# A decoder trunk on one core: the two compressions of a sparse attention done as one, and new constants in the clock that orders TensorE's work

## The chip, the cores and the metric

The kernel runs on 1 core of one Trainium2 chip. The metric is the device time in microseconds, lower is better. Three runs of the kernel before took 1984.06 to 1987.67 us, with a median of 1984.88 us.

## The reference

Four decoder layers over 256 positions of width 1024, float32. Each layer is a half-step SwiGLU FFN (width 2816), a token mixer, and a second FFN, each between RMS norms with a residual. Layers 0 and 3 have windowed attention, layer 2 a block attention, and layer 1 the sparse attention that the change touches. Its compressed branch makes one key and one value out of every 32 positions (stride 16, 15 blocks, 4 groups of heads):

```python
def compress_kv(kv, pos, w1, w2):
    B, S, G, dh = kv.shape                       # 1, 256, 4, 64
    n_cmp = (S - CMP_LEN) // CMP_STRIDE + 1      # 15
    idx = jnp.arange(n_cmp)[:, None] * CMP_STRIDE + jnp.arange(CMP_LEN)[None, :]
    blocks = kv[:, idx] + pos[:, None, :]
    flat = blocks.transpose(0, 1, 3, 2, 4).reshape(B, n_cmp, G, CMP_LEN * dh)
    return jax.nn.gelu(flat @ w1) @ w2           # w1: 2048 x 256, w2: 256 x 64

kc_b = compress_kv(kc, cmp_pos[0], cmp_w1[0], cmp_w2[0])
vc_b = compress_kv(vc, cmp_pos[1], cmp_w1[1], cmp_w2[1])
# p_cmp = masked_softmax(q . kc_b);  o_cmp = p_cmp @ vc_b
# o = g0 * o_cmp + g1 * o_selected + g2 * o_window
```

## The kernel before, in words

**Two chains.** The 256 positions are two tiles of 128 rows, and each has a chain of steps (class `Chain`, t = 0 and 1) through all four layers. A step is a Python generator's stretch between two `yield`s, and the steps of the two chains are laid one behind the other on TensorE. Both chains use the same weights: a slab (1 MB, two halves of 128x1024 floats) serves chain 0 and then chain 1.

**Weights.** Every half is loaded by SyncE into one of four `raw` buffers, and split: ScalarE writes `hi` (rounded to fp32r), VectorE writes `lo` = raw - hi. A product with a slab half is then x_hi*hi, x_hi*lo and x_lo*hi; 12 products of 512 columns are one visit of a chain to a slab. `hi` and `lo` go into a pool of 28 slots (`SLOTS`, `k4`), which the attention's tiles share. `plan.held` counts the slots that four users hold (chain 0, chain 1, the keys and values, and the compression, which is number 3), `plan.want` what is reserved for them, and `room()` what is left; `feed()` splits the next half only where two slots are left and 1.2 us (`PACE`) have passed on the rough clock.

**The rough clock.** TensorE's order is the order in which the program emits its instructions (`manual_schedule`), and `choose()` decides it: among the steps of the two chains and of the helpers that are running, the one whose inputs are ready first, ties going to the lower rank (the compression has rank -1, chain 0 rank 0, chain 1 rank 1, the compressed core rank 1.5). What is ready when comes from class `Clock`: every emitted instruction moves it on by a fixed duration that stands in `TimedProducts.matmul` (L226) and `Engines` (L252 to L257). The orders on ScalarE, VectorE and SyncE come from the compiler's own scheduler, which takes the emitted order as priority. An instruction of TensorE that is placed too early waits on the chip, and all behind it waits too.

**The sparse layer** (`attn_b`, L888). Each chain projects queries, gates and six kinds of keys and values (ten visits and a product of 48 columns), then runs `core`: eight jobs of four heads, in each the scores (`acc<-k,k`), a maximum on VectorE, exp on ScalarE, transposes (`trp`), and the product with the values (`pv`). When chain 1 has the first half of its keys, `compress()` (L946) is started beside the cores. It takes the keys (s = 0), and then the values (s = 1): four adds on VectorE lay out the blocks in `xf` (`k<-k,post`), 16 products of 256 columns with w1 come in four steps of four (`hid`; the weights `k<-w` come in quarters, each into a slot), then a GELU of seven instructions on 64 partitions, two transposes (`hidT`), and the small second product (`kcb`, `vcb`). When both are there, `cmp_core` (L849) of both chains may go on (`scc`, `trc`, `pvc`).

A float32 product is two records on TensorE, one fp32r product or one transpose is one. A hidden product has 64 output rows: it uses half of the array's columns (the form `128*64`).

Of the kernel before, what the change touches and what calls it, by code (L numbers as in the profile page):

```python
# [214 lines left out]
class TimedProducts:  # L215
# [7 lines left out]
    def matmul(self, out, lhs, rhs, share=1.0, **kw):  # L223
        c, n = self.clock, free_size(rhs)
        self.begin(out, lhs, rhs)
        c.now += share * (max(0.107, n / 2372) if rhs.dtype == F32R else max(0.213, n / 600))  # L226
        c.passed(c.now, [out], [lhs, rhs])
        self.engine.matmul(out, lhs, rhs, **kw)  # L228

# [21 lines left out]
class Engines:  # L251
    def __init__(self, nc, clock):  # L252
        self.tensor = TimedProducts(nc.tensor, clock)
        self.scalar = Timed(nc.scalar, "act", clock, 0.06, 0.00083)
        self.vector = Timed(nc.vector, "dve", clock, 0.065, 0.00105)
        self.gpsimd = Timed(nc.gpsimd, "pool", clock, 0.45, 0.001)
        self.sync = TimedLoads(nc.sync, clock)  # L257
# [3 lines left out]
def trunk(ctx: ExitStack, tc: tile.TileContext, x, rel, gains, pre, sinks, pos, w1, w2, wts, hot,  # L261
# [43 lines left out]
    def drop(who, n=1):  # L305
        plan.held[who] -= n

    def k2(shape, dtype=F32):
        return p2.tile(shape, dtype, tag="k2", name="k2")
# [103 lines left out]
    class Chain:  # L413
# [474 lines left out]
        def attn_b(self, i):  # L888
            t = self.t
            r, r8 = self.r_and_r8()  # L890
            if t == 0:
                shared["cmp"] = False
                shared["cT"] = [k4(2, [P, 4, SEQ]) for _ in range(2)]
                shared["kT"] = k4(2, [P, 2, 2, SEQ])
                shared["v"] = k4(2, [P, 2, 2, 256])
            kT, vs = shared["kT"], shared["v"]
            yield from self.queries(r8)
            p = yield from self.project(48)
            gate = self.small("gate", 48)
            rh = self.small("rh")  # L900
            nc.vector.tensor_scalar_mul(rh, r, 0.5)
            nc.scalar.activation(gate, p[:, :48], AF.Tanh, scale=rh)
            nc.vector.tensor_scalar(gate, gate, 1.0, 0.5, op0=ALU.add, op1=ALU.mult)
            gate = gate.rearrange("p (h b) -> p b h", b=3)
            yield free_bank(), True
            p = yield from self.project(512)
            for s in range(2):
                self.keys_dup(p[:, s * 256:(s + 1) * 256], r, shared["cT"][s])
            yield from self.turns()
            plan.want[t] = 3 + 2 * t  # L910
            for s in range(2):
                p = yield from self.project(512)
                self.keys(p[:, :256], r, kT[:, s, :, t * P:(t + 1) * P])
                nc.scalar.activation(vs[:, t, s, :], p[:, 256:], AF.Copy, scale=r)
                if t == 0 and s == 0:
                    plan.want[3] = 3
                yield from self.turns(s == 1)
                if t and s == 0:
                    start(compress(), FIRST)
            o = k4(t, [P, D])  # L920
            branches = [(lambda h, s=s: kT[:, s, h // 8, :],
                         lambda h, kb, s=s: vs[:, kb, s, (2 * (h // 8) + h % 2) * DH:
                                               (2 * (h // 8) + h % 2 + 1) * DH],
                         gate[:, s + 1, :]) for s in range(2)]
            self.oc = k4(t, [P, D])
            self.cmp = False
            start(self.cmp_core(gate[:, 0, :]), CMP_CORE)
            yield from self.core(o, branches, 0)
            while not self.cmp:
                yield clock.now + 0.5, False  # L930
            for q in range(2):
                c = slice(q * 512, (q + 1) * 512)
                nc.vector.tensor_add(o[:, c], o[:, c], self.oc[:, c])
            drop(t)
            self.leave(3)
            yield from self.out_proj(o, i)
# [8 lines left out]

    def compress():  # L946

        vbd = k4(2, [P, 2, 8, DH])
        nc.vector.memset(kcb, 0.0)
        hv = k2([P, 2, 2, 4, 32])  # L950
        for s in range(2):
            src = shared["cT"][s]
            xf = k4(3, [P, 16, 4, 16])
            nc.vector.memset(xf[:, :, :, NCMP:], 0.0)
            view = src.rearrange("p g (n j b) -> p j g n b", j=8, b=2)
            for e in range(2):
                rows = slice(DH * e, DH * e + DH)
                for m in range(2):
                    nc.vector.tensor_tensor(
                        xf[rows, 8 * m:8 * m + 8, :, :NCMP], view[rows, :, :, m:m + NCMP, e],  # L960
                        post[rows, s, 8 * m:8 * m + 8].unsqueeze(2).unsqueeze(3)
                        .broadcast_to([DH, 8, 4, NCMP]), op=ALU.add)
            drop(2)
            plan.want[2] -= 1
            ws = []
            for q in range(2):
                w = k4(3, [P, HALF])
                nc.sync.dma_start(w, w1[2 * s, :, q * HALF:(q + 1) * HALF])
                ws.append(w)
            p = bank([64, 2, P], "hid")  # L970
            for q in range(4):
                w = ws[q]
                yield when(w, xf), False
                for j in range(4 * q, 4 * q + 4):
                    at = (j % 4) * CMP_HIDDEN
                    nc.tensor.matmul(p.rearrange("p c n -> p (c n)"),
                                     xf[:, j].rearrange("p g n -> p (g n)"),
                                     w[:, at:at + CMP_HIDDEN], start=j == 0, stop=j == 15)
                drop(3)
                if q < 2:  # L980
                    w = k4(3, [P, HALF])
                    nc.sync.dma_start(w, w1[2 * s + 1, :, q * HALF:(q + 1) * HALF])
                    ws.append(w)
            drop(3)
            hid = k2([64, 2, P])
            q = k2([64, 2, P])
            nc.scalar.activation(q, p, AF.Square)
            nc.vector.tensor_scalar(q, q, 0.044715, 1.0, op0=ALU.mult, op1=ALU.add)
            nc.vector.tensor_tensor(q, q, p, op=ALU.mult)
            nc.scalar.activation(q, q, AF.Tanh, scale=GELU_C)  # L990
            nc.vector.tensor_scalar(q, q, 1.0, 0.5, op0=ALU.add, op1=ALU.mult)
            nc.vector.tensor_tensor(hid, q, p, op=ALU.mult)
            yield max(when(hid), free_bank()), False
            p = bank([P, 2, 64], "hidT")
            for c in range(2):
                nc.tensor.transpose(p[:, c, :], hid[:, c, :], ident[:64, :64])
            hid = k2([P, 2, 64])
            nc.vector.tensor_copy(hid, p)
            if s == 0:
                yield max(when(hid), free_bank()), False  # L1000
                p = bank([P, 64], "kcb")
                for c in range(2):
                    nc.tensor.matmul(p, w2s[:, 0, c].rearrange("p a d -> p (a d)"), hid[:, c, :],
                                     start=c == 0, stop=c == 1)
                for e in range(2):
                    rows = slice(DH * e, DH * e + DH)
                    nc.vector.tensor_copy(
                        kcb[rows, :, e, :],
                        p[rows, :].rearrange("p (g e n) -> p g e n", e=2, n=16)[:, :, e, :])
            else:  # L1010
                for c in range(2):
                    nc.vector.tensor_copy(
                        hv[:, c], hid[:, c, :].rearrange("p (g n) -> p g n", n=32).unsqueeze(2)
                        .broadcast_to([P, 2, 4, 32]))
                for G in range(2):
                    yield max(when(hv), free_bank()), False
                    p = bank([P, DH], "vcb")
                    for c in range(2):
                        nc.tensor.matmul(p, hv[:, c, G].rearrange("p a n -> p (a n)"),
                                         w2s[:, 1, c, 0, :], start=c == 0, stop=c == 1)  # L1020
                    nc.vector.tensor_tensor(vbd[:, G], p.unsqueeze(1).broadcast_to([P, 8, DH]),
                                            bm.unsqueeze(2).broadcast_to([P, 8, DH]), op=ALU.mult)
        shared["vbd"] = vbd
        plan.want[3] = 0
        shared["cmp"] = True
# [84 lines left out]
```

## Time and profile before

| what | value |
|---|---|
| median of three runs | 1984.88 us (1984.06 to 1987.67) |
| profiled execution | 1989.9 us |
| its span, first to last instruction | 1988.1 us |
| TensorE busy, share of the span | 1947.6 us, 98% |
| VectorE busy, share | 1236.2 us, 62% |
| ScalarE busy, share | 1040.7 us, 52% |
| GpSimd busy, share | 37.1 us, 2% |
| mean granted TensorE clock | 0.996 |

Products overlap in the records (one of 512 columns is shown with 389 ns, and the next starts 227 ns after it), so TensorE's busy share says where it waited long, and not how close to its peak it is. What a product costs is read from the start of one to the start of the next.

### The profile page before, as it was taken

To read this page: it belongs to the slowest core of one execution; us is meant where nothing else is said; L and a number is where in the kernel's file an instruction comes from. 1 tells how busy PE (TensorE), PEld (TensorE's weight loads), DVE (VectorE), ACT (ScalarE), POOL (GpSimd) and SP (SyncE) were. 2 spreads that over 40 slices of the span, in tenths; PEclk is the share of its full clock that TensorE was granted. 3 is DMA by queue.
4 is the path that set the end of the run, shared out by engine and by line. 5 is a ranking of instruction groups with operands and counts; after the bars stand their busy time and mean duration, and the time that the engine had idled before them with its cause. 6 is when DMAs were issued, how large, how long until landed. Compare 5 with 4: busy or idle time off the path is not lost. (4 is left out here: it accounts for less than half of the span.)

```text
span 1988.1 us, 27346 instructions
## 1 busy us (share of the span) xinstructions
PE 1947.6 (98%) x9948; PEld 1589.5 (80%) x9948; DVE 1236.2 (62%) x2271; ACT 1040.7 (52%) x1886; POOL 37.1 (2%) x62
## 2 busy tenths in 40 slices
PE   7999999999999999999999999999999999999998
PEld 6778878888888886788888887778888888878886
DVE  6556676556655648765566556466556655667553
ACT  6445665445544555554455446565445544665442
POOL 0000000000000000000000000000000000000000
PEclk9999999999999999999999999999999999999999
DMA  8578556555555454365555555556555555536551
GB/s 265 172 230 238 173 143 199 190 188 184 191 190 191 141 180 109 119 199 191 185 183 193 188 184 179 178 147 201 184 186 186 195 185 185 177 106 207 188 184 57
DMA packets 114099, 356.42 MB, mean 179 GB/s; under 512 B 12811, under 2 KB 30475, under 8 KB 113964
## 3 DMA queue, kind: packets, MB, share of 16 engines
q1 hardware_dynamic: 113964, 354.68, 55.3%
q8 instruction: 78, 1.28, 0.2%
q14 instruction: 57, 0.47, 0.1%
HBM read 352.01 MB, written 2.62 MB: 178 GB/s over the span
## 5 line engine op out<-in xcount | busy, mean ns | idle before, releaser
L210 DVE TENSOR_TENSOR lo<-raw,hi 128x1024 fp32r<-128x1024 f32 x625 | 761.0, 1223 | 378.0 <-ACT hi L210 346.9
L210 ACT ACTIVATE hi<-raw 128x1024 fp32r<-128x1024 f32 x625 | 660.6, 1064 | 383.4 <-PE acc L228 202.1
L228 PE MATMUL proj<-hi,xh 128*128 128x512 f32 (+1 forms) x1696 | 675.7, 400 | 2.6 <-DVE xl L210 1.9
L228 PE MATMUL proj<-lo,xh 128*128 128x512 f32 (+1 forms) x1696 | 658.7, 389 | 0.8 <-DVE lo L210 0.8
L228 PE MATMUL proj<-hi,xl 128*128 128x512 f32 (+1 forms) x1696 | 449.2, 387 | 0.0
L228 PEld LDWEIGHTS proj<-hi,xh 128*128 128x128 f32 x1696 | 320.6, 189 | 64.4 <-ACT xh L210 3.0
L228 PEld LDWEIGHTS proj<-lo,xh 128*128 128x128 f32 x1696 | 321.2, 189 | 61.5 <-DVE lo L210 1.1
L228 PEld LDWEIGHTS proj<-hi,xl 128*128 128x128 f32 x1696 | 316.2, 188 | 67.7
L228 PE MATMUL acc<-hi,hh 128*128 128x512 f32 x704 | 219.5, 393 | 3.0 <-ACT hh L210 3.0
L228 PE MATMUL acc<-lo,hh 128*128 128x512 f32 x704 | 217.7, 390 | 0.0
L228 PE MATMUL acc<-hi,hl 128*128 128x512 f32 x704 | 188.8, 390 | 0.0
L210 ACT ACTIVATE h<-proj,rh 128x256 f32<-128x256 f32 x176 | 82.0, 466 | 189.7 <-PE proj L228 189.6
L210 ACT ACTIVATE hh<-trh 128x256 fp32r<-128x256 f32 x176 | 66.9, 380 | 177.7 <-PE trh L235 177.6
L228 PEld LDWEIGHTS acc<-hi,hh 128*128 128x128 f32 x704 | 131.3, 189 | 30.1 <-ACT hh L210 3.7
L228 PEld LDWEIGHTS acc<-lo,hh 128*128 128x128 f32 x704 | 132.7, 189 | 27.9
L228 PEld LDWEIGHTS acc<-hi,hl 128*128 128x128 f32 x704 | 132.2, 188 | 27.7
L210 DVE SCALAR_TENSOR_TENSOR h<-h,proj 128x256 f32<-128x256 f32 x176 | 73.6, 418 | 120.0 <-ACT h L210 119.9
L210 DVE TENSOR_TENSOR hl<-trh,hh 128x256 fp32r<-128x256 f32 x176 | 73.9, 420 | 112.2 <-ACT hh L210 112.2
L210 ACT ACTIVATE k<-k,nm 128x128 f32<-128x128 f32 (+1 forms) x160 | 70.7, 446 | 35.8 <-DVE nm L210 35.7
L210 DVE SCALAR_TENSOR_TENSOR h<-proj,c,h 128x256 f32<-128x256 f32 x176 | 85.0, 483 | 5.2
L235 PE MATMUL trh<-ident,h 128*128 128x128 f32 x352 | 67.0, 272 | 0.0
L235 PEld LDWEIGHTS trh<-ident,h 128*128 128x128 f32 x352 | 48.7, 139 | 22.4 <-PE tab L228 0.6
(100 smaller groups left out, 1116.3 us busy)
## 6 DMA issues: line engine op xcount, KB each, us to landing
raw<-wts SPq DMA_DIRECT2D x624, 512.0 KB, 4.5
bias<-scratch SPq DMA_DIRECT2D x96, 128.0 KB, 5.0
g<-gains SPq DMA_DIRECT2D x12, 512.0 KB, 4.9
k<-w SPq DMA_DIRECT2D x8, 512.0 KB, 6.0
scratch<-k SPq DMA_DIRECT2D x4, 384.0 KB
out<-x SPq DMA_DIRECT2D x4, 256.0 KB, 2.1
x<-x SPq DMA_DIRECT2D x2, 256.0 KB
x<-x SPq DMA_DIRECT2D x1, 512.0 KB
```

The costliest lines, as they stand in the source:

```text
L210: return call(out, *args, **kw)
L228: self.engine.matmul(out, lhs, rhs, **kw)
L235: self.engine.transpose(out, src, ident)
```

## The change

The two compressions are done together, and the first product in two parts. Both layouts `xf` are made first (eight adds), and each part takes half of w1's rows for keys and values: 16 products, one for the keys and one for the values in turn, into the two halves of a bank's partitions. The rough clock counts each with half of its duration (`share=0.5`). The first part's sums are copied out by ScalarE, the second's added to them by VectorE; then one GELU runs on 128 partitions, with two transposes of 128x128, and the second products as before. The compression may now hold 6 slots (two `xf` and four quarters) in place of 3. The waits for the inputs come once for each part, with all four quarters.

In the rough clock an fp32r product of 512 columns goes from 0.2158 to 0.2268 us, a float32 one of 256 columns from 0.4267 to 0.4324 us, and an instruction of ScalarE on 1024 columns from 0.910 to 0.964 us. VectorE's, GpSimd's and the loads' constants stay.

```diff
@@ class TimedProducts
-        c.now += share * (max(0.107, n / 2372) if rhs.dtype == F32R else max(0.213, n / 600))
+        c.now += share * (max(0.112, 0.0135 + n / 2400) if rhs.dtype == F32R else max(0.22, n / 592))
@@ class Engines
-        self.scalar = Timed(nc.scalar, "act", clock, 0.06, 0.00083)
+        self.scalar = Timed(nc.scalar, "act", clock, 0.07, 0.000873)
@@ attn_b
                 if t == 0 and s == 0:
-                    plan.want[3] = 3
+                    plan.want[3] = 6
@@ compress
         hv = k2([P, 2, 2, 4, 32])
+        xfs = []
         for s in range(2):
             src = shared["cT"][s]
             xf = k4(3, [P, 16, 4, 16])
...
+            xfs.append(xf)
             drop(2)
             plan.want[2] -= 1
-            ws = []
-            for q in range(2):
+        ws = []
+
+        def quarter(q):
+            for s in range(2):
                 w = k4(3, [P, HALF])
-                nc.sync.dma_start(w, w1[2 * s, :, q * HALF:(q + 1) * HALF])
+                nc.sync.dma_start(w, w1[2 * s + q // 2, :, q % 2 * HALF:(q % 2 + 1) * HALF])
                 ws.append(w)
-            p = bank([64, 2, P], "hid")
-            for q in range(4):
-                w = ws[q]
-                yield when(w, xf), False
-                for j in range(4 * q, 4 * q + 4):
-                    at = (j % 4) * CMP_HIDDEN
-                    nc.tensor.matmul(p.rearrange("p c n -> p (c n)"),
-                                     xf[:, j].rearrange("p g n -> p (g n)"),
-                                     w[:, at:at + CMP_HIDDEN], start=j == 0, stop=j == 15)
-                drop(3)
-                if q < 2:
-                    w = k4(3, [P, HALF])
-                    nc.sync.dma_start(w, w1[2 * s + 1, :, q * HALF:(q + 1) * HALF])
-                    ws.append(w)
-            drop(3)
-            hid = k2([64, 2, P])
...
+        sums = []
+        for m in range(2):
+            quarter(2 * m)
+            quarter(2 * m + 1)
+            yield max(when(*ws[4 * m:], *xfs), free_bank()), False
+            p = bank([P, 2, P], "hid")
+            for j in range(8):
+                at = (j % 4) * CMP_HIDDEN
+                for s in range(2):
+                    nc.tensor.matmul(p[HALVES[s]].rearrange("p c n -> p (c n)"),
+                                     xfs[s][:, 8 * m + j].rearrange("p g n -> p (g n)"),
+                                     ws[4 * m + j // 4 * 2 + s][:, at:at + CMP_HIDDEN], share=0.5,
+                                     start=j == 0, stop=j == 7)
+            drop(3, 4)
+            sums.append(k2([P, 2, P]))
+            if m:
+                nc.vector.tensor_tensor(sums[1], sums[0], p, op=ALU.add)
+            else:
+                nc.scalar.activation(sums[0], p, AF.Copy)
+        drop(3, 2)
+        hid, q = sums
+        nc.scalar.activation(hid, q, AF.Square)
+        nc.vector.tensor_scalar(hid, hid, 0.044715, 1.0, op0=ALU.mult, op1=ALU.add)
+        nc.vector.tensor_tensor(hid, hid, q, op=ALU.mult)
+        nc.scalar.activation(hid, hid, AF.Tanh, scale=GELU_C)
+        nc.vector.tensor_scalar(hid, hid, 1.0, 0.5, op0=ALU.add, op1=ALU.mult)
+        nc.vector.tensor_tensor(hid, hid, q, op=ALU.mult)
+        yield max(when(hid), free_bank()), False
+        p = bank([P, 2, P], "hidT")
+        for c in range(2):
+            nc.tensor.transpose(p[:, c, :], hid[:, c, :], ident)
+        hid = k2([P, 2, 64])
+        nc.vector.tensor_copy(hid, p[:, :, :64])
+        for c in range(2):
+            nc.vector.tensor_copy(
+                hv[:, c], p[:, c, 64:].rearrange("p (g n) -> p g n", n=32).unsqueeze(2)
+                .broadcast_to([P, 2, 4, 32]))
...
```

## Rows read from the trace of the kernel before

**Rows 1.** The page's first lines: the span and the engines' busy time.

```profile
span 1988.1 us, 27346 instructions
PE 1947.6 (98%) x9948; PEld 1589.5 (80%) x9948; DVE 1236.2 (62%) x2271; ACT 1040.7 (52%) x1886; POOL 37.1 (2%) x62
```

**Rows 2.** Busy time by stretches of 100 us. Columns: the stretch, its length, then for PE, PEld, DVE, ACT and POOL the busy us and the count, the granted clock of TensorE, the DMA share and GB/s. The first stretch holds only FFNs, the second most of the sparse layer.

```profile
500.00:600.00 100.00, 100.00 (x452) 82.26 (x451) 61.23 (x74) 48.76 (x61) 0.00 (x0) 1.00 0.59 193
700.00:800.00 100.00, 96.27 (x831) 74.49 (x829) 69.16 (x271) 57.98 (x176) 4.37 (x6) 0.98 0.45 134
```

**Rows 3.** The same by 10 us, in the sparse layer.

```profile
680.00:690.00 10.00, 9.98 (x45) 8.22 (x45) 8.08 (x19) 7.82 (x19) 0.55 (x1) 0.83 0.54 178
750.00:760.00 10.00, 9.29 (x108) 7.11 (x108) 9.20 (x45) 6.56 (x29) 0.72 (x1) 1.00 0.09 36
760.00:770.00 10.00, 8.74 (x57) 5.34 (x57) 9.87 (x43) 4.46 (x16) 0.73 (x1) 1.00 0.52 142
820.00:830.00 10.00, 7.64 (x32) 5.94 (x33) 8.57 (x27) 5.78 (x21) 1.27 (x2) 0.83 0.22 66
```

**Rows 4.** Groups of TensorE's instructions by line and shape: the hidden products. Columns: count, then busy us and mean ns of one, then the idle time before them and what ended it.

```profile
L228 PE MATMUL hid<-k,k 128*64 128x256 f32 x64 | 15.1, 383 | 1.6 <-PE trp L235 0.9 <-DMA k<-w 0.7
```

**Rows 5.** TensorE's instructions in order of time while the compression runs. Columns: start us, us until the group's end, engine, line, operation, tiles, form, count, and the idle time before it.

```profile
736.94 1.94 PE L228 MATMUL hid<-k,k 128*64 128x256 f32 x8
...
745.87 3.67 PE L228 MATMUL hid<-k,k 128*64 128x256 f32 x16
749.47 0.44 PE L235 MATMUL trp<-ident,k 128*128 128x128 f32 x2
...
761.17 3.64 PE L228 MATMUL hid<-k,k 128*64 128x256 f32 x16 [0.86 <-PE trp L235]
...
765.80 0.66 PE L235 MATMUL trp<-ident,k 128*128 128x128 f32 x4 [0.40 <-DVE k L210]
...
770.73 1.94 PE L228 MATMUL hid<-k,k 128*64 128x256 f32 x8 [0.72 <-DMA k<-w]
```

**Rows 6.** The same view: a group of products on half of the array's columns (`128*64`), one on half of its rows (`64*128`), and what starts behind each.

```profile
773.18 1.15 PE L228 MATMUL pv<-k,pT 128*64 128x64 f32 x32
774.27 0.66 PE L235 MATMUL trp<-ident,k 128*128 128x128 f32 x4
...
776.06 1.14 PE L228 MATMUL acc<-k,k 64*128 64x256 f32 x8
777.02 0.28 PE L235 MATMUL hidT<-ident,k 64*128 64x64 f32 x2
```

**Rows 7.** The chain of work that ended last, in order of time: start us, us until the next piece, what. Fp32r products of 512 columns.

```profile
1808.32 2.72 PE proj L228 x12
1811.04 0.87 PE trx L235 x8
```

**Rows 8.** VectorE's instructions in order of time, about the adds that lay out the blocks.

```profile
731.37 3.83 DVE L210 TENSOR_TENSOR k<-k,post 64x480 f32<-64x480 f32 x4
...
759.13 2.82 DVE L210 TENSOR_TENSOR k<-k,post 64x480 f32<-64x480 f32 x3
761.96 0.29 DVE L210 CUSTOM_DVE_ANT_0 k<-acc,bias 128x128 f32<-128x128 f32 x1
```

**Rows 9.** Groups of VectorE's instructions by shape: the layout adds, the GELU on 64 partitions, and an instruction of its size on 128 partitions.

```profile
L210 DVE TENSOR_TENSOR k<-k,post 64x480 f32<-64x480 f32 x8 | 7.5, 972 | 0.0
...
L210 DVE TENSOR_TENSOR k<-k,hid 64x256 f32<-64x256 f32 x4 | 1.6, 409 | 0.1
...
L210 DVE TENSOR_SCALAR k<-k 64x256 f32<-64x256 f32 x4 | 1.1, 278 | 0.7 <-ACT k L210 0.7
...
L210 DVE TENSOR_TENSOR k<-k,nmc 128x256 f32<-128x256 f32 x2 | 0.8, 414 | 0.0
```

**Rows 10.** SyncE's queue in order of time: the issues of loads about the compression.

```profile
725.57 0.43 SPq L248 DMA_DIRECT2D k<-w  x1
...
744.50 3.67 SPq L248 DMA_DIRECT2D k<-w  x3
...
764.06 0.38 SPq L248 DMA_DIRECT2D k<-w  x1
```

**Rows 11.** Loads by kind: count, KB each, median us from issue to landing.

```profile
raw<-wts SPq DMA_DIRECT2D x624, 512.0 KB, 4.5
...
k<-w SPq DMA_DIRECT2D x8, 512.0 KB, 6.0
```

**Rows 12.** Who TensorE waited for in the whole span: us in total, times, longest us.

```profile
PE trx L235 <- DVE x L210: 6.4, 11, 2.0
...
PE acc L228 <- ACT hh L210: 3.0, 2, 2.6
```

**Rows 13.** The split of a weight half, from the page's groups.

```profile
L210 DVE TENSOR_TENSOR lo<-raw,hi 128x1024 fp32r<-128x1024 f32 x625 | 761.0, 1223 | 378.0 <-ACT hi L210 346.9
L210 ACT ACTIVATE hi<-raw 128x1024 fp32r<-128x1024 f32 x625 | 660.6, 1064 | 383.4 <-PE acc L228 202.1
```

**Rows 14.** TensorE in order of time in the first stretch of rows 3: what ran before the granted clock fell, then the first of eight products, and the ninth.

```profile
680.71 1.09 PE L235 MATMUL trx<-ident,x 128*128 128x128 f32 x8
681.82 0.77 PE L228 MATMUL proj<-hi,xh 128*128 128x512 f32 x1
...
685.35 0.85 PE L228 MATMUL proj<-hi,xl 128*128 128x512 f32 x3
```

More of the change, by code (lines that the diff above doesn't have):

```diff
@@ L984, in compress @@
-            drop(3)
-            hid = k2([64, 2, P])
[L986 to L993, printed above, removed]
@@ L994, in compress @@
-            p = bank([P, 2, 64], "hidT")
-            for c in range(2):
[L996 to L1022, printed above, removed]
@@ new lines, in compress @@
+        for c in range(2):
[6 more added lines that the diff above has]
+                .broadcast_to([P, 2, 4, 32]))
+        yield max(when(hid), free_bank()), False
+        p = bank([P, 64], "kcb")
+        for c in range(2):
+            nc.tensor.matmul(p, w2s[:, 0, c].rearrange("p a d -> p (a d)"), hid[:, c, :],
+                             start=c == 0, stop=c == 1)
@@ new lines, in compress @@
+        for e in range(2):
+            rows = slice(DH * e, DH * e + DH)
+            nc.vector.tensor_copy(
+                kcb[rows, :, e, :],
+                p[rows, :].rearrange("p (g e n) -> p g e n", e=2, n=16)[:, :, e, :])
+        for G in range(2):
+            yield max(when(hv), free_bank()), False
+            p = bank([P, DH], "vcb")
+            for c in range(2):
+                nc.tensor.matmul(p, hv[:, c, G].rearrange("p a n -> p (a n)"),
+                                 w2s[:, 1, c, 0, :], start=c == 0, stop=c == 1)
+            nc.vector.tensor_tensor(vbd[:, G], p.unsqueeze(1).broadcast_to([P, 8, DH]),
+                                    bm.unsqueeze(2).broadcast_to([P, 8, DH]), op=ALU.mult)
```

## The prediction, made before the changed kernel ran

> **What bounds the kernel now.** I read the page's head first, then the busy time by stretches, TensorE's waits, and the sparse layer's order of time on TensorE, VectorE and SyncE. TensorE is busy for 98% of the span [rows 1], and in a stretch of FFNs for all of it, with VectorE at 61% [rows 2]: no other engine can be the bound there, and only less work on TensorE or a shorter wait of it can move the end. The reader is to see where those waits are. The sparse layer holds TensorE at 96.3 of 100 us [rows 2], and inside it, while the compression runs, at 9.29 and 8.74 of 10 us with VectorE at 9.20 and 9.87 [rows 3]. So in this place two engines are nearly full at once: time taken from TensorE counts in full only if VectorE doesn't take the bound over.
>
> **The change, part by part.**
>
> *The hidden products.* They are 64 records [rows 4]. Sixteen in a row take from 745.87 to 749.47, 3.60 us or 0.225 each [rows 5], so all 64 hold TensorE for 14.4 us. Each uses half of the columns. Where two products on half of the array meet, the trace shows them side by side: eight records on half of the rows with the same 256 columns take from 776.06 to 777.02, 0.96 us or 0.24 a pair, and 32 records on half of the columns take 1.09 us, 0.034 each [rows 6]. After the change 64 records are 32 pairs: 7.2 us at 0.225, 7.7 at 0.24. I take 7.5, so -6.9. The upper end is no gain at all: the pairs on half of the columns in these rows stream the same values twice, and no row shows two column halves that stream different data, as keys' and values' w1 are.
>
> The Trainium skill, page "TensorE: Matmul & The Clock Gate", section "Measured speedup vs the span model", gives three column tiles 2.38 times and not 3 times the speed, which speaks against a full halving. By it, as an estimate, the pairs would take 14.4/(2 x 0.79) = 9.1 us and the gain would be 5.3. The row with 0.24 a pair disagrees for halves of the rows and shows nothing for halves of the columns with two streams.
>
> *Waits that go.* The values' first products wait 0.86 us, a transpose behind them 0.40 for VectorE's work, and the last quarter 0.72 for its load [rows 5]. The first two lie where VectorE lays out the values' blocks, in a row that ends at 761.95 [rows 8]; that work moves to the front, so both go: -1.3. The third I keep: the second part's four quarters can only be issued when the first part gives its slots back. Now three quarters are issued at 744.50 and nothing of the values is needed before 761.17 [rows 5, 10]; afterwards four of them follow one another, each 6.0 us from issue to landing [rows 11], with both cores' work as cover. Between 0 and 3 us, I take the 0.7 that stands there now: 0.
>
> *The adds at the front.* Four adds take VectorE from 731.37 to 735.20 [rows 8]; the first product starts at 736.94 [rows 5]. Eight in one go take twice 3.83, to 739.0, and the scores' maxima of the cores queue behind them, so TensorE finds neither the product nor the next scores ready from 736.94 on. The rough clock prices such an add at 0.065 + 480 x 0.00105 = 0.57 us where the trace has 0.97 [rows 9], so it will place the product some 3 us too early. The wait is 2.1 us for the adds and some maxima behind them; bounds 0 (if a visit to a slab covers it) and 3.8 (the four added adds in full). I take +2.5.
>
> *The GELU.* Eight instructions of VectorE on 64 partitions (4 x 0.409 + 4 x 0.278 = 2.75 us) become four of the same width on 128, which cost the same each (0.414 at 128x256 against 0.409 at 64x256) [rows 9]; with one more add of 0.41 and the copies VectorE is left with about 1 us less, and ScalarE about the same. The keys' result waits for the values', but what needs it has the lowest rank. Off the sum: 0, bounds -1 and 0.
>
> *Three more slots.* They are 1.5 halves of weights that are split later, from the keys' projection to the compression's end. A half costs 1.06 on ScalarE and 1.22 on VectorE [rows 13], and each visit of 12 products takes 2.72 us [rows 7], so there is time to split while the other chain works; but chain 0 ends its projections a visit later, and one visit less covers its first core job. Bounds 0 and 2.7, I take +0.5.
>
> *The rough clock.* Twelve products take 2.72 us, 0.2267 each [rows 7]: the new 0.2268 is right, the old 0.2158 was 5% short. ScalarE's 0.964 for 1024 columns still falls short of 1.064, and VectorE's 1.14 of 1.223 [rows 13]. In the FFNs TensorE has no idle time to win [rows 2]. What the order could win or lose elsewhere is of the size of the waits at the norms and transposes: 6.4 us in 11 waits and 3.0 in two [rows 12]. If a third of these went, -3; if as many steps came as much too early, +3. I take 0, for TensorE's steps get longer in the clock while VectorE's stay too short, which works both ways.
>
> *Not touched.* Eight products after 681.82 take 3.53 us in place of 1.82 (0.2267 each), at the lower level of 1.2 GHz, for the granted clock is 0.83 in that stretch; transposes and products of 48 columns come before it [rows 3, 7, 14]. That is 1.7 us, and this work stays; that another such stretch comes or goes is part of the range.
>
> **Sum.** -6.9 - 1.3 + 0 + 2.5 + 0 + 0.5 + 0 = -5.2 us. The profiled execution took 1989.9 us, so it would take 1984.7. That execution stands 5.0 above the median of 1984.88; the difference is applied to the median: 1979.7 us.
>
> **Rivals.**
>
> *The halves don't run side by side.* For it: their streams differ, see above. Against it: both forms of half products pair up wherever they meet [rows 6]. The sum is then without the -6.9: +1.7, or 1986.6 us, with TensorE later than the rough clock thinks.
>
> *VectorE keeps the gain.* It is at 9.20 and 9.87 of 10 us there [rows 3], the adds come in one block, and what leaves TensorE leaves a hole. With the upper bounds of the adds (3.8) and of the slots (2.7) the sum is -6.9 - 1.3 + 3.8 + 2.7 = -1.7, so 1983.2 us. Against it: VectorE's work there is partly splitting of weights, which can move.
>
> *Slower: SyncE's queue.* The four quarters of a part stand in the queue one behind the other and wait for slots; a weight load behind them cannot pass. The layer's output and the next FFN live on these loads. If the four raw buffers run empty, the next halves come as a series: 4.5 us for the landing [rows 11], then 1.06 + 1.22 for each split [rows 13], and for four halves 13.6 us; the sum becomes +8.4 and the time 1993.3 us. It decides from the point where the wait for slots is longer than the four buffers last, four halves at 2.72 us for both chains together, 10.9 us. Against it: the quarters already stand in that queue, and weight loads pass between them [rows 10].
>
> **Numbers.** Some 0.2%, 4 us, is what a measurement of this kernel can tell from no change. The forecast, a gain of over 4 us (below 1980.9), gets 0.57, the order's luck included; VectorE keeping the gain 0.21 and the unpaired halves 0.12, together 0.33 within 4 us; the queue, or as much lost by the order at other places, 0.10. The forecast's own range goes down to 1972 (-5.2, less 2.5 for no wait at the adds, 0.5 for the slots, 3 from the order and 1.7 for one low-clock stretch: -12.9) and up to 1980.9. The whole range must take in the first two rivals, which end at 1986.6: 1971.5 to 1987.5, leaving out the queue and a little below.
>
> **What would show it.** Right: the hidden products in two groups of 32 records, pairs starting within some 10 ns, a group under 4 us; TensorE idle before the first for 2 to 3 us with VectorE's adds as the releaser; no wait at the values' layout; VectorE with eight adds in a row; FFN stretches unchanged with 100% and the same count. Wrong: a group of 32 records that takes 7 us (no pairing); a wait of TensorE for `lo` or `hi` near the layer's output (slots or queue); waits at `trx` and `trh` in other layers that differ by more than 3 us in all (the rough clock has moved steps). The forecast is wrong in size if the first wait is above 4 us, or if the order elsewhere turns out to weigh more than the compression.

## The result, and the profile after

The changed kernel takes 2002.86 us (median of four runs, 2002.08 to 2003.13) against 1986.28 us for the kernel before on the same chip: a ratio of 1.0083, with a 95% interval from 1.0070 to 1.0096. It is slower by some 16 us; the forecast was a gain of 5. The profiled execution took 2003.1 us.

The page's first lines, which answer to [rows 1]:

```profile
span 2001.3 us, 27325 instructions
PE 1950.9 (97%) x9946; PEld 1591.8 (80%) x9946; DVE 1233.8 (62%) x2267; ACT 1039.1 (52%) x1885; POOL 39.5 (2%) x62
```

TensorE is busy 3.3 us longer than in [rows 1], although 7 us of it should have gone, and its span is 13.2 us longer: about 10 us are new idle time. Most of the missing busy time is the clock: the granted clock is at its lower level, 1.2 GHz, for 32.0 us of this execution and for 16.0 of the one before (mean 0.992 and 0.996). Half of the work is lost at that level (eight products took 3.53 us in place of 1.82 [rows 14]), so by this estimate 8 us more are lost to it than before. To find where, both traces are cut at the same places of the work, the middle of each FFN, found by counting the 7440 fp32r products of 512 columns. The stretches of the changed kernel, one row for each, with the columns of [rows 2]: the first attention layer (A) with half an FFN on either side, the norm between two FFNs with the other halves (F1), the sparse layer (B), F2, the block attention (C), F3, and the last attention layer (A2).

```profile
111.39:385.26 273.87, 269.11 (x1447) 220.86 (x1446) 178.17 (x359) 153.77 (x305) 4.38 (x8) 0.99 0.62 192
385.26:575.17 189.91, 187.94 (x853) 154.03 (x852) 117.43 (x168) 95.53 (x142) 3.04 (x4) 1.00 0.56 186
575.17:936.12 360.95, 346.62 (x2039) 281.01 (x2038) 226.66 (x523) 187.04 (x398) 13.51 (x16) 0.98 0.50 161
936.12:1125.63 189.51, 187.92 (x853) 154.03 (x852) 117.44 (x168) 95.35 (x142) 3.04 (x4) 1.00 0.57 186
1125.63:1435.37 309.74, 305.19 (x1605) 250.39 (x1604) 187.94 (x354) 168.53 (x314) 5.23 (x8) 0.99 0.57 180
1435.37:1624.83 189.46, 187.95 (x854) 154.02 (x853) 117.44 (x168) 95.33 (x142) 3.05 (x4) 1.00 0.57 186
1624.83:1900.82 275.99, 272.59 (x1448) 220.91 (x1446) 173.81 (x356) 150.38 (x302) 4.38 (x8) 0.99 0.52 170
```

Three stretches of the kernel before, in the same columns (A, F1, B):

```profile
114.80:383.80 269.00, 266.12 (x1448) 218.23 (x1447) 177.44 (x359) 153.36 (x305) 4.38 (x8) 1.00 0.64 196
383.80:571.61 187.81, 187.56 (x854) 154.07 (x852) 118.01 (x168) 95.35 (x142) 3.04 (x4) 1.00 0.57 188
571.61:930.62 359.01, 350.42 (x2041) 282.28 (x2040) 226.89 (x527) 188.11 (x399) 10.21 (x16) 0.99 0.51 162
```

In F1 the instructions are the same, and the second number shows TensorE idle for 2.0 us (189.91 - 187.94) where it was idle for 0.3. In B, TensorE's busy time falls by 3.8 us, where the joint compression alone lets it fall by 8.4 (342.05 us in e2, below), and the stretch is 1.9 longer. The lengths in profiled executions, with three of the experiments (us; start and end are what lies outside):

| kernel | start | A | F1 | B | F2 | C | F3 | A2 | end | span |
|---|---|---|---|---|---|---|---|---|---|---|
| before | 114.8 | 269.0 | 187.8 | 359.0 | 187.8 | 310.7 | 187.8 | 270.6 | 100.5 | 1988.1 |
| after | 111.4 | 273.9 | 189.9 | 360.9 | 189.5 | 309.7 | 189.5 | 276.0 | 100.5 | 2001.3 |
| e1, constants alone | 111.6 | 273.8 | 189.9 | 362.5 | 189.5 | 309.1 | 189.5 | 272.6 | 100.5 | 1998.9 |
| e2, compression alone | 112.5 | 269.4 | 187.9 | 350.5 | 187.8 | 311.6 | 187.9 | 271.7 | 100.5 | 1979.8 |
| e17, after with a margin | 110.7 | 270.3 | 188.2 | 349.6 | 187.9 | 308.8 | 187.8 | 271.0 | 100.5 | 1974.9 |

Between before and after, A and A2 are 10.3 us longer, the three F stretches 5.4, B 1.9, and the rest shorter by 4.4. Who TensorE waited for in the changed kernel, to be read against [rows 12]:

```profile
PE trx L235 <- DVE x L210: 13.0, 14, 2.1
...
PE acc L228 <- DVE mx L210: 5.4, 5, 2.3
PE hid L228 <- DMA k<-w: 3.6, 4, 1.7
...
PE acc L228 <- ACT hh L210: 0.9, 2, 0.5
```

The norms' transposes (`trx`) wait 14 times for 13.0 us in place of 11 times for 6.4, and the hidden products wait four times for their weights. What happens in A, in order of time on TensorE:

```profile
235.08 0.66 PE L235 MATMUL trp<-ident,k 128*128 128x128 f32 x4
238.01 1.33 PE L228 MATMUL acc<-k,k 64*128 64x128 f32 x8 [2.27 <-DVE mx L210]
239.27 0.79 PE L228 MATMUL proj<-hi,xh 128*128 128x512 f32 x1
...
243.59 0.69 PE L228 MATMUL pv<-k,pT 128*64 128x64 f32 x16
```

A step of the core comes 2.27 us before its maximum is ready (the kernel before waits 0.2 us for `mx` in all of A), and right behind that wait the granted clock is at its lower level, 1.2 GHz, for 3.4 us: the 12 products from 239.27 take 4.3 us in place of the 2.72 of [rows 7]. A second such stretch of 3.4 us stands at 276, and A2 has one of 6.8; the kernel before has none in either layer. The wait (2.1 more) and 1.6 for each of the two stretches make 5.3, an estimate that covers A's 4.9 us.

### The profile page after: what moved, and what is told of

Same layout as the page of the kernel before. It is cut to its first block, busy times and chain, and to the rows that moved or that the text cites. A ratio compares the mean times of both kernels' runs of the same rounds, so it can differ in the third digit from the quotient of the medians.

```text
span 2001.3 us, 27325 instructions
## 1 busy us (share of the span) xinstructions
PE 1950.9 (97%) x9946; PEld 1591.8 (80%) x9946; DVE 1233.8 (62%) x2267; ACT 1039.1 (52%) x1885; POOL 39.5 (2%) x62
## 5 line engine op out<-in xcount | busy, mean ns | idle before, releaser
L210 POOL TENSOR_TENSOR r<-v,mhalf 128x1 f32<-128x1 f32 x48 | 32.5, 678 | 1840.5 <-DVE v L210 1840.5
```

The costliest lines, as they stand in the source:

```text
L210: return call(out, *args, **kw)
```

## The experiments

**Which part?** e1 has the new constants alone, e2 the joint compression alone.

```diff
e1, against before:
-        c.now += share * (max(0.107, n / 2372) if rhs.dtype == F32R else max(0.213, n / 600))
+        c.now += share * (max(0.112, 0.0135 + n / 2400) if rhs.dtype == F32R else max(0.22, n / 592))
-        self.scalar = Timed(nc.scalar, "act", clock, 0.06, 0.00083)
+        self.scalar = Timed(nc.scalar, "act", clock, 0.07, 0.000873)
e2: the changed kernel with these two lines as they were before
```

> The kernel before with the new constants of the rough clock alone (TensorE's and ScalarE's); the compression is the old one. Theory A (the constants move TensorE's steps in all layers, and that costs more than the compression gains): 8 to 18 us slower than before, with waits of TensorE at the norms' transposes near 13 us in place of 6.4. Theory B (the joint compression costs the time, by late loads and the low clock behind it; the constants do little): within 4 us of before.

> The changed kernel with the old constants: the joint compression alone. Theory A: 2 to 8 us faster than before, as the sum of the prediction has it for this part. Theory B: 8 to 18 us slower than before.

e1 measured 1.0065 [1.0052, 1.0079] times before, e2 0.9974 [0.9962, 0.9985]. So the constants cost some 13 us, and the joint compression gains 5.2 (0.0026 of 1987 us), as the sum said. The compression in e2, TensorE in order of time:

```profile
732.59 3.67 PE L228 MATMUL hid<-k,k 128*64 128x256 f32 x32
736.19 0.72 PE L228 MATMUL acc<-k,k 64*128 64x128 f32 x8
...
739.18 2.00 PE L228 MATMUL acc<-k,k 64*128 64x128 f32 x16 [1.68 <-DVE mx L210]
...
745.35 3.67 PE L228 MATMUL hid<-k,k 128*64 128x256 f32 x32
```

32 records take from 732.59 to 736.19, 3.60 us: as long as 16 took [rows 5]. The halves with two different streams pair in full. The hidden products don't wait; the scores' maxima behind the adds do, 1.68 us. The two together would make +8 us, and the changed kernel is 16 slower. Most of what is missing lies in B, where e2 gains 8.5 us (359.0 to 350.5) and the changed kernel none.

**Which constant?** e3 has TensorE's line alone, e4 ScalarE's alone, both on the kernel before; e12 is e2 with ScalarE's line.

> The kernel before with TensorE's new constants alone. Theory A in the form that TensorE's longer steps make the order too early for VectorE, whose constants stay short: 8 to 18 us slower than before, as with both. In the form that ScalarE's constants move the order: within 4 us of before. Theory B: within 4 us.

> The kernel before with ScalarE's new constants alone. If TensorE's constants are the cause: within 4 us of before. If ScalarE's are: 8 to 18 us slower. If both orders are only as good as chance, each of the two lands somewhere between 5 us faster and 12 us slower, and the two don't add up to the run with both.

> The change without TensorE's constants: joint compression and ScalarE's new constants. Theory S, with TensorE's constants as the cause: 2 to 8 us faster than before, as the joint compression alone. If the sparse layer is slow wherever the order differs from that run's: 5 us slower than before or more, in that layer.

e3: 1.0105 [1.0092, 1.0119]; e4: 0.9996 [0.9987, 1.0005]; e12: 1.0010 [0.9998, 1.0023]. TensorE's constant is the cause of the loss of e1, and it is the one that the trace bears out best (0.2268 against 0.2267 measured). ScalarE's does nothing by itself. In B it goes either way: beside the joint compression it takes the gain away (350.5 us in e2, 359.3 in e12), beside TensorE's constant it gives 10 us back (372.6 in e3, 362.5 in e1).

**Too long against what?** If a longer TensorE step lets the clock's other durations fall behind, lengthening one of those must repair it. In the changed kernel e5 gives every instruction of the other engines 0.1 us more before it starts, e6 makes VectorE's and GpSimd's durations 5% longer, e13 VectorE's alone, and e9 raises GpSimd's fixed part by half.

```diff
e5:  -    LAG = 0.1
     +    LAG = 0.2
e13: -        self.vector = Timed(nc.vector, "dve", clock, 0.065, 0.00105)
     +        self.vector = Timed(nc.vector, "dve", clock, 0.0683, 0.001104)
e6:  as e13, and
     -        self.gpsimd = Timed(nc.gpsimd, "pool", clock, 0.45, 0.001)
     +        self.gpsimd = Timed(nc.gpsimd, "pool", clock, 0.473, 0.00105)
e9:  the gpsimd line alone, 0.45 -> 0.68
```

> The changed kernel with the rough clock's delay between two engines (LAG) at 0.2 in place of 0.1 us. Theory S (with TensorE's steps at their true length the clock's delays between engines are too short beside them, so steps are laid with too little cover): 10 to 20 us faster than the changed kernel, 2 to 8 us faster than before, and the stretches of FFNs back at 187.8 us from 189.5. Theory L (the order turns on ties, and any constant gives another order, better or worse): as likely to stay within 5 us of the changed kernel as not.

> The changed kernel with VectorE's and GpSimd's constants made 5% longer too, so that the three engines keep the proportion that they had before. Theory S in the form that VectorE's share is what matters: within 5 us of the joint compression alone (0.997 of before). If it is the delay between engines or the loads' and the pace's constants: still 10 to 20 us slower than before. Theory L: anywhere between.

> The changed kernel with GpSimd's constant alone at what the trace shows, 0.68 in place of 0.45 us; it has one instruction in every norm between two FFNs. Theory S (a norm that the clock takes for too short is laid with one visit of cover in place of two): the FFN stretches back from 189.5 to 187.8 us and the first attention layer's from 273.9 to about 269, 8 to 12 us faster than the changed kernel in all, with the sparse layer left at some 361. Theory L (ties): no stretch returns to its value of before as a rule.

> The changed kernel with VectorE's constants alone made 5% longer. If VectorE's is the constant that orders the steps about the norms: FFN stretches back at 187.8 us and the first attention layer at 269, 6 to 15 us faster than the changed kernel. If it takes GpSimd's too: FFN stretches stay at 189.5.

e5: 1.0072 [1.0057, 1.0087]; e6: 1.0005 [0.9995, 1.0015]; e9: 1.0060 [1.0038, 1.0081]; e13: 0.9992 [0.9977, 1.0006]. VectorE's constant alone takes back the whole loss against before; GpSimd's does nothing that stands clear of the noise. F1 and F2 of e13:

```profile
383.56:571.37 187.81, 187.56 (x854) 154.08 (x852) 118.05 (x168) 95.34 (x142) 3.04 (x4) 1.00 0.57 188
924.17:1112.11 187.94, 187.61 (x854) 154.07 (x852) 117.94 (x168) 95.36 (x142) 3.04 (x4) 1.00 0.57 188
```

They are as they were before the change. e5 repairs them too (188.5, 187.9 and 188.0 us), but not B (362.8) and C (316.6).

**A slope or a step?** On e2, e7 goes half the way with TensorE's constant (an fp32r product of 512 columns 0.2214 us), e8 goes the other way (0.2048).

```diff
e7: -        c.now += share * (max(0.107, n / 2372) if rhs.dtype == F32R else max(0.213, n / 600))
    +        c.now += share * (max(0.109, n / 2313) if rhs.dtype == F32R else max(0.216, n / 596))
e8: n / 2372 -> n / 2500
```

> The joint compression with TensorE's constants half way to the new ones (0.2213 us for an fp32r product of 512 columns), ScalarE's as before. Theory S: between the joint compression alone (0.997 of before) and TensorE's full constants, some 5 to 10 us slower than the first. Theory L: no order in it; it may also be the fastest or the slowest.

> The joint compression with TensorE's constant moved the other way, 0.2048 us for an fp32r product of 512 columns, 10% under what the trace shows. Theory S: more cover for every delay, so not slower than the joint compression alone by more than 3 us. Theory L: 5 us or more away from it, on either side.

e7: 0.9977 [0.9968, 0.9987]; e8: 0.9962 [0.9948, 0.9977]. Half the step costs nothing of the 13 us, and neither does a step in the wrong direction: it is no slope but a comparison that turns somewhere in the last half. The place is seen at a norm between two FFNs. The transposes there on TensorE, in the kernel before:

```profile
1018.35 1.23 PE L235 MATMUL trx<-ident,x 128*128 128x128 f32 x8 [0.24 <-DVE x L210]
...
1022.18 0.38 PE L235 MATMUL trh<-ident,h 128*128 128x128 f32 x2
...
1041.74 1.04 PE L235 MATMUL trx<-ident,x 128*128 128x128 f32 x8
```

In the changed kernel:

```profile
1023.96 1.23 PE L235 MATMUL trx<-ident,x 128*128 128x128 f32 x8 [0.35 <-DVE x L210]
...
1035.92 0.38 PE L235 MATMUL trh<-ident,h 128*128 128x128 f32 x2
...
1048.97 1.23 PE L235 MATMUL trx<-ident,x 128*128 128x128 f32 x8 [1.24 <-DVE x L210]
```

The first `trx` is chain 0's norm. Before, chain 1's next `trh` follows 3.8 us later, behind 12 products; after, 12.0 us later, for 36 products of chain 0 have come between. So chain 1's last products, and its own norm behind them, move towards the end of the work that should cover that norm, and the second `trx` waits 1.24 us for VectorE.

The rough clock's own numbers (the program's estimate while it lays the order, no times of the chip) show the turn. Chain 0's next step, a yield at the end of `boundary`, is ready 0.13 us after the 12 products of chain 1 that end there; with the new constant these 12 take 12 x 0.011 = 0.13 us longer, and the two are ready at the same moment, 0.00 apart. Ties go to the lower rank, chain 0. With e13's VectorE they are 0.17 apart again, for VectorE's work lies before chain 0's step. With e9's GpSimd they stay at 0.00, for its instruction comes before the norm's transposes, from which both times run.

The same comparison, worked out in the rough clock of every kernel of this text, sorts them all. It is 0.00 in the changed kernel, e1, e3, e9 and e11, at the end of every FFN that another step follows, and in these F1 takes 189.9 to 190.1 us and A 272.9 to 275.3. It is 0.06 in e7, 0.10 in e5, 0.13 to 0.26 in the kernel before and the others, and there F1 takes 187.8 to 188.5 us and A 268.9 to 271.0, but for e5 with 273.0 in A.

**The one comparison.** If that is the cause, moving that one readiness alone must repair it. e17 is the changed kernel, both new constants in it, with one number added:

```diff
-            yield when(self.xl[0]), True
+            yield when(self.xl[0]) + 0.2, True
```

> The changed kernel with one readiness in the rough clock 0.2 us later: the first residue after a norm, by which a chain's next visit is laid. If that one comparison is what costs the FFN stretches: back from 189.5 to 187.8 us, and 5 us or more faster than the changed kernel in all. If the loss comes from many small shifts: FFN stretches stay above 189 us.

e17: 1977.77 us (1975.15 to 1979.39), 0.9947 [0.9927, 0.9967] times before. The same norm:

```profile
1006.62 1.23 PE L235 MATMUL trx<-ident,x 128*128 128x128 f32 x8 [0.29 <-DVE x L210]
1010.43 0.38 PE L235 MATMUL trh<-ident,h 128*128 128x128 f32 x2
...
1030.01 1.04 PE L235 MATMUL trx<-ident,x 128*128 128x128 f32 x8
```

`trh` is back at 3.8 us, the second `trx` waits no more, and by the table the F stretches, A (270.3) and A2 (271.0) are back within 1.4 us of before and B is at 349.6. This kernel is faster than both the one before and the changed one, the latter by some 25 us. Some 11 of these are the clock, by the same estimate: its profiled execution has 9.4 us at the lower level, the changed kernel's 32.0.

**What is left in B.** In the changed kernel the hidden products stand in pieces, TensorE in order of time:

```profile
742.89 0.62 PE L228 MATMUL hid<-k,k 128*64 128x256 f32 x2 [0.75 <-DMA k<-w]
...
744.15 1.95 PE L228 MATMUL hid<-k,k 128*64 128x256 f32 x16 [0.64 <-DMA k<-w]
...
746.59 1.94 PE L228 MATMUL hid<-k,k 128*64 128x256 f32 x14 [0.49 <-DMA k<-w]
...
763.11 1.73 PE L228 MATMUL hid<-k,k 128*64 128x256 f32 x13 [1.68 <-DMA k<-w]
```

They wait 3.6 us for quarters of w1. SyncE's queue in the changed kernel, and then in e2 (start, us until the group's end):

```profile
733.69 1.46 SPq L248 DMA_DIRECT2D raw<-wts  x2
735.21 2.36 SPq L248 DMA_DIRECT2D k<-w  x4
```

```profile
715.56 2.01 SPq L248 DMA_DIRECT2D raw<-wts  x2
717.62 2.71 SPq L248 DMA_DIRECT2D k<-w  x4
```

In both kernels the same 243 weight loads stand before the quarters, but in the changed kernel the last two of them go out 18 us later (13 counted from where B starts), and the quarters behind them. They wait for the buffers of two halves that ScalarE splits only at 731.32, behind results of the projections. ScalarE in the changed kernel:

```profile
729.38 0.84 ACT L210 ACTIVATE k<-proj,r 128x256 f32<-128x256 f32 x2 [6.90 <-PE proj L228]
730.11 1.36 ACT L210 ACTIVATE k<-trq 128x512 f32<-128x512 f32 x3
731.32 2.04 ACT L210 ACTIVATE hi<-raw 128x1024 fp32r<-128x1024 f32 x2
```

In e2 the two splits stand at 713.22 and 714.90. e11 issues the quarters on GpSimd's queue in the changed kernel; e14, e15, e16 and e18 do it in e12, e6, e8 and e17. e10 is the kernel before with the six slots alone.

```diff
e11: +        self.quarters = TimedLoads(nc.gpsimd, clock)
     -                nc.sync.dma_start(w, w1[2 * s + q // 2, :, q % 2 * HALF:(q % 2 + 1) * HALF])
     +                nc.quarters.dma_start(w, w1[2 * s + q // 2, :, q % 2 * HALF:(q % 2 + 1) * HALF])
e10: -                    plan.want[3] = 3
     +                    plan.want[3] = 6
```

> The kernel before with 6 slots reserved for the compression in place of 3, nothing else. The prediction's term for the slots: 0 to 2.7 us slower, with 0.5 taken. If the reservation is what holds weight loads in front of the quarters and so costs the changed kernel its sparse layer: 5 to 10 us slower, in that layer.

> The changed kernel with the compression's eight quarter loads issued on GpSimd's queue in place of SyncE's. If the quarters come late because they stand behind weight loads that wait for their buffers: TensorE's waits for the quarters (3.6 us) go, the hidden products start within 2 us of the end of the projections, and the sparse layer falls from 360.9 to some 354 us. If the layer is long because of the order on TensorE: less than 2 us change there.

> Joint compression and ScalarE's new constants, the eight quarters on GpSimd's queue. If late quarters are the whole difference to the joint compression alone: the sparse layer falls from 359.3 to 350 to 353 us and the time to 0.997 of before. If the order of the cores' steps is part of it: 355 us or more.

> The changed kernel with VectorE's and GpSimd's constants 5% longer and the quarters on GpSimd's queue. If late quarters and the norms' cover are all that was lost: 0.997 of before, the sparse layer at 350 to 353 us. If the layer's order is a matter of ties: 355 us or more in it, and no gain over before.

> The joint compression with TensorE's constant at 0.2048 us, and the quarters on GpSimd's queue. That order has no wait for the quarters, so within 3 us of it (0.9962 of before), unless the free queue lets weight loads start earlier: then 3 us or more faster.

> The same with the eight quarters on GpSimd's queue. If that comparison and the late quarters are all that the change lost: 0.997 to 1.000 of before, no wait for the quarters, the sparse layer at 355 us or less. If the first attention layers' order is a loss of its own: still 1.002 or more.

e10: 1.0004 [0.9989, 1.0018], so the slots cost nothing that can be told. e11: 1.0065 [1.0050, 1.0080], B 358.4 us; e14: 0.9980 [0.9966, 0.9994], B 355.9 against 359.3 in e12; e15: 0.9997 [0.9984, 1.0011]; e16: 0.9968 [0.9955, 0.9981]; e18: 0.9969 [0.9954, 0.9984], B 353.0 against 349.6 in e17. In e11 the first four quarters go out at 724.02, ahead of the two weight loads:

```profile
724.02 2.35 POOL L248 DMA_DIRECT2D k<-w  x4 [28.79 <-ACT k L210]
```

The wait for `k<-w` is gone from TensorE's waits there, and B falls by 2.5 us only. Nor do the other pairs follow the quarters: e15's B is 3.7 us shorter than e6's (355.2 against 358.9), although TensorE waits for no quarter in e6, and e18 loses 3.4. What differs as well is how long TensorE is at its lower level in B. B less half of that time is an estimate of B at the full clock (profiled executions, us):

| kernel | B | at the lower level in B | B less half of it | waits for quarters |
|---|---|---|---|---|
| before | 359.0 | 10.2 | 353.9 | 0.7 |
| after | 360.9 | 13.7 | 354.1 | 3.6 |
| e12 | 359.3 | 10.2 | 354.2 | 3.4 |
| e2 | 350.5 | 10.2 | 345.4 | 0 |
| e6 | 358.9 | 23.9 | 346.9 | 0 |
| e11 | 358.4 | 17.1 | 349.9 | 0 |
| e15 | 355.2 | 17.1 | 346.6 | 0 |
| e17 | 349.6 | 3.4 | 347.9 | 0 |
| e18 | 353.0 | 17.1 | 344.5 | 0 |

With the joint compression the estimate is 344 to 350 us in every kernel that doesn't wait for quarters (e2, e6 to e8, e11, e13 to e18), and 354 to 358 in every one that does (the changed kernel, e5, e9, e12). So late quarters go with some 8 us of B, more than the 3.6 that TensorE waits for them, and the rest of what B varies by is mostly the clock. Why the planner lays the two splits late, and what else comes with them, was not settled.

## Why the prediction was wrong

**The hidden products (-6.9) and the waits that go (-1.3): right.** 64 records take 7.1 us in e2 (3.60 and 3.51), 7.5 was taken. The Trainium skill, page "TensorE: Matmul & The Clock Gate", section "Measured speedup vs the span model", would by its shortfall have given 9.1, as the prediction's estimate says; the row disagrees, two halves with different streams pair without loss. The values' waits at 761.17 and 765.80 are gone from e2.

**The adds at the front (+2.5): right in place, a little large.** It is 1.7 us in e2, at the scores, not at the hidden products.

**The quarters (0, bounds 0 to 3): too low in the changed kernel.** 3.6 us of waits there, none in e2, and some 8 us of B by the estimate above. The rival named SyncE's queue, but the wrong way round: weight loads didn't stand behind the quarters, the quarters stood behind weight loads that waited for their buffers.

**The three slots (+0.5): nothing** that e10 could tell; **the GELU (0):** not seen apart.

**The sum without the rough clock** was -5.2 us; e2 measured -5.2 (by its interval -3.0 to -7.6). Some of this agreement is luck: in e2's profiled execution B alone is 8.5 shorter, more than the terms give, and C and A2 are 0.9 and 1.1 longer.

**The rough clock: the step that failed.** "I take 0, for TensorE's steps get longer in the clock while VectorE's stay too short, which works both ways." Alone it costs 13 us, four times the bound of 3. The working looked at the waits that stood in the trace [rows 12] and asked what share of them could go or come. It saw "In the FFNs TensorE has no idle time to win" and put no loss there. But a norm whose transposes don't wait is covered by a margin that no view of the trace shows: 0.13 us on the rough clock, which 12 products of 0.011 us more use up. The sentence before it had the reason in hand, that VectorE's constant stays 7% short (1.14 for 1.223): TensorE's true steps were now compared with VectorE's short ones, and chain 0's norm seemed done too early. e13 shows that by lengthening VectorE, e17 by moving the one readiness. With the late quarters, which also come from the order, the account roughly closes: -5.2 and 13 and some 8 make the 16 us that were measured.

**What one turned comparison costs.** e17 moves it at every norm, so it shows what all of them cost together. The three F stretches lose 1.6 to 2.1 us each, of which 1.24 is the wait shown; A and A2 lose 5 each, where a step too early brings a wait and behind it products at the lower clock. e17 gives nearly all of these back. In A2 only 1 to 2 us belong to the comparison for certain: e1, e3, e9 and e11, in which it is turned too, lose no more there and have no stretch at the lower level. The forecast gave 0.10 to the queue "or as much lost by the order at other places"; it was the order, by a little at each of many norms, and the late quarters as well. The test named at its end, waits at `trx` and `trh` that differ by more than 3 us in all, was met: `trx` alone waits 13.0 us for 6.4 [rows 12].

## What to carry to other kernels

In a planner that compares estimated times, what matters is the difference of two sums: setting one engine's constant right while the others stay short moves every difference between its sums and theirs the same way. Correcting VectorE's along with it took the loss back here (e13, e6), but truer constants were not the faster ones: the old constants (e2, 0.9974) and wronger ones (e8, 0.9962) did no worse than e13 (0.9992). So before touching a constant, print which choices are won by less than the change adds up to over a step, and give those a margin; here 0.2 us on one readiness was worth some 25. And when a change has two parts, time each alone: the half that was meant as bookkeeping cost more than twice what the other gained.

## What the runs showed of the hardware

Two float32 products of 256 columns on the two column halves, with different data streaming, take as long together as one alone: 32 records took 3.60 us in e2, as 16 did before [rows 5], 0.225 us for a pair of records, of which a product has two.

The quarters, 512 KB each, take a median of 6.0 us from issue to landing in the kernel before, up to three at a time [rows 10, 11], and with the joint compression 7.4 (e2) to 9.1 us (e12) on SyncE's queue, where four are issued together. On GpSimd's queue it is 5.6 to 6.2 us in e11, e14 and e16, but 8.3 in e15 and 8.6 in e18, so the queue alone doesn't set it. From the page's DMA issues, the changed kernel, e11 and e18:

```profile
k<-w SPq DMA_DIRECT2D x8, 512.0 KB, 8.0
```

```profile
k<-w POOLq DMA_DIRECT2D x8, 512.0 KB, 5.6
```

```profile
k<-w POOLq DMA_DIRECT2D x8, 512.0 KB, 8.6
```

The granted clock also fell with TensorE hardly idle. The changed kernel by 10 us, columns as in [rows 3], and the products of 32 columns across the fall:

```profile
770.00:780.00 10.00, 9.43 (x108) 8.15 (x105) 9.96 (x39) 3.93 (x9) 0.00 (x0) 0.91 0.39 113
780.00:790.00 10.00, 10.00 (x86) 8.48 (x84) 7.65 (x36) 4.99 (x19) 0.83 (x1) 0.58 0.37 100
```

```profile
775.73 1.97 PE L228 MATMUL scc<-kcb,k 128*128 128x32 f32 x16 [0.57 <-DVE k L210]
...
780.08 3.46 PE L228 MATMUL scc<-kcb,k 128*128 128x32 f32 x16
```

From 778.1 on TensorE runs at its lower level for 10.2 us, with 1.1 us idle in the ten before: both cores' compressed scores stand close together here, with small products and transposes between. In e2 the clock falls for 10.2 us at the same work, at 762.1, and so it does in e8 and e11. But what stands close together doesn't decide it alone. In e17 the two groups come in the same order, 3.5 us apart, with the same 0.6 us of waiting before the first, and the clock doesn't fall:

```profile
760.95 1.97 PE L228 MATMUL scc<-kcb,k 128*128 128x32 f32 x16 [0.58 <-DVE k L210]
...
764.43 1.94 PE L228 MATMUL scc<-kcb,k 128*128 128x32 f32 x16
```

In the kernel before, where products of 256 columns lie between them, both groups take less than 2 us as well:

```profile
784.81 1.97 PE L228 MATMUL scc<-kcb,k 128*128 128x32 f32 x16
...
791.25 1.87 PE L228 MATMUL scc<-kcb,k 128*128 128x32 f32 x16
```

What sets off the fall is open.
